# One activation table set at the head of the program instead of two in turn: a prefix log-sum-exp scan on one core

## The chip, the core and the metric

The kernel runs on one core of one Trainium2 chip. The metric is the device time of one execution in microseconds, as the median of several runs. ScalarE is called ACT here, VectorE DVE, TensorE PE (PEld for its weight loads), GpSimd POOL, SyncE SP; ACTq and SPq are the instruction queues of ACT and SP where they issue transfers.

## The reference

For each of 8 batches and 2048 columns, the output at row t is the log-sum-exp of the input rows 0 to t:

```python
B, S, D = (8, 4096, 2048)
out[:, 0, :] = x[:, 0, :]
for t in range(1, S):
    mx = np.maximum(out[:, t - 1, :], x[:, t, :])
    out[:, t, :] = mx + np.log(np.exp(out[:, t - 1, :] - mx) + np.exp(x[:, t, :] - mx))
```

Input and output are float32, 268.4 MB each.

## The kernel before, in words

The kernel takes exp of the input, makes running sums over rows with matmuls against triangular matrices of ones, and takes the logarithm of the sums. A block is 256 rows of one batch: 128 partitions with two neighbouring rows each, so a tile of 128 x 4096 numbers, 2 MB in float32. There are 16 blocks in a batch and 128 in all. The outer loop goes over pairs of batches, the middle loop over the 16 blocks, and the inner loop alternates between the two batches of the pair, each with its own running sum in PSUM (`ps`, 128 x 2048 float32).

One block goes through these steps, with the line numbers of the profile:

- L58: SP issues the load of the block into `xt` (pool of four buffers).
- L61: ACT takes Exp of all 4096 columns of `xt` into `et` (bf16, four buffers). When it is done, the `xt` buffer is free and SP can issue a load into it.
- L65 and L69: PE adds the sums up to each even row to `ps`, four pairs of matmuls of 128 x 512.
- L75: ACT takes Ln of `ps` into the first half of `ot` (float32, four buffers), the even rows.
- L76: DVE adds the odd rows' `et` to `ps` and writes the second half of `ot`.
- L77: ACT takes Ln of that half in place.
- L79: ACT issues the store of the block from `ot`. An `ot` buffer is free again when its store has landed.
- L84 and L88: PE adds the rest of the block to `ps`, so that `ps` carries the sum over the whole block. It waits for L76, which reads `ps` before.

The four triangular matrices `Li`, `Ls`, `Ui` and `Us` are made once by POOL.

ACT works in order. The order of its instructions is set by the tile scheduler when the program is built; in the middle of the program it repeats every three blocks. It ends with the last Exp, the store of the third block from the end, Ln of `ps` for the last two blocks, and then Ln in place and the store for each of the two. Exp and Ln are taken from different activation table sets in this program, so an ACT_TABLE_LOAD stands wherever ACT goes from one function to the other. These loads are not written in the source; they carry the line of the ACTIVATE behind them.

Of the kernel before, what the change touches and what calls it, by code (L numbers as in the profile page):

```python
# [1 line left out]

# [4 lines left out]


@with_exitstack
def kernel(  # L10
    ctx: ExitStack,
    tc: tile.TileContext,
    x: bass.AP,
    out: bass.AP,
):
    nc = tc.nc
    f32 = mybir.dt.float32
    bf16 = mybir.dt.bfloat16
    ACT = mybir.ActivationFunctionType

    B, S, D = x.shape
    P = 128
    SB = 256
    NBLK = S // SB
    FD = 512
    NC = D // FD
    PAIR = 2

    const = ctx.enter_context(tc.tile_pool(name="const", bufs=1))
    Li = const.tile([P, P], bf16)  # L30
    masks.make_upper_triangular(nc, Li, val=1.0, diag=True)
    Ls = const.tile([P, P], bf16)
    masks.make_upper_triangular(nc, Ls, val=1.0, diag=False)
    Ui = const.tile([P, P], bf16)
    masks.make_lower_triangular(nc, Ui, val=1.0, diag=False)
    Us = const.tile([P, P], bf16)
    masks.make_lower_triangular(nc, Us, val=1.0, diag=True)

    xpool = ctx.enter_context(tc.tile_pool(name="xpool", bufs=4))
    epool = ctx.enter_context(tc.tile_pool(name="epool", bufs=4))  # L40
    opool = ctx.enter_context(tc.tile_pool(name="opool", bufs=4))
    ppool = ctx.enter_context(tc.tile_pool(name="ppool", bufs=1, space=bass.MemoryType.PSUM))

    x_v = x.rearrange("b (k p two) d -> b k p (two d)", p=P, two=2)
    o_v = out.rearrange("b (k p two) d -> b k p (two d)", p=P, two=2)

    for bp in range(0, B, PAIR):
        psums = [
            ppool.tile([P, D], f32, name=f"ps_{bp}_{j}", tag=f"ps{j}")
            for j in range(PAIR)  # L50
        ]
        for k in range(NBLK):
            for j in range(PAIR):
                b = bp + j
                ps = psums[j]

                xt = xpool.tile([P, 2 * D], f32)
                nc.sync.dma_start(out=xt, in_=x_v[b, k])  # L58

                et = epool.tile([P, 2 * D], bf16)  # L60
                nc.scalar.activation(et, xt, ACT.Exp)  # L61

                for c in range(NC):
                    lo, hi = c * FD, (c + 1) * FD
                    nc.tensor.matmul(  # L65
                        ps[:, lo:hi], Li, et[:, lo:hi],
                        start=(k == 0), stop=False, skip_group_check=True,
                    )
                    nc.tensor.matmul(  # L69
                        ps[:, lo:hi], Ls, et[:, D + lo : D + hi],  # L70
                        start=False, stop=False, skip_group_check=True,
                    )

                ot = opool.tile([P, 2 * D], f32)
                nc.scalar.activation(ot[:, :D], ps, ACT.Ln)  # L75
                nc.vector.tensor_add(ot[:, D:], ps, et[:, D:])  # L76
                nc.scalar.activation(ot[:, D:], ot[:, D:], ACT.Ln)  # L77

                nc.scalar.dma_start(out=o_v[b, k], in_=ot)  # L79

                if k < NBLK - 1:
                    for c in range(NC):
                        lo, hi = c * FD, (c + 1) * FD
                        nc.tensor.matmul(  # L84
                            ps[:, lo:hi], Ui, et[:, lo:hi],
                            start=False, stop=False, skip_group_check=True,
                        )
                        nc.tensor.matmul(  # L88
                            ps[:, lo:hi], Us, et[:, D + lo : D + hi],
                            start=False, stop=False, skip_group_check=True,  # L90
                        )


# [1 line left out]
_INS = ['x']  # L95
_OUTS = [((8, 4096, 2048), 'float32')]


# [23 lines left out]
```

## Time and profile before

| | |
|---|---|
| time, median of 3 runs | 1329.4 us (1328.58 to 1329.96) |
| span of the profiled execution | 1326.9 us |
| ACT busy | 1268.8 us, 96% |
| PE busy | 654.6 us, 49% |
| DVE busy | 289.3 us, 22% |
| moved between HBM and SBUF | 537.22 MB, 405 GB/s over the span |
| share of the 16 DMA engines: loads, stores | 51.4%, 47.3% |

The span goes from the first to the last instruction of one profiled execution. The three timed runs lie 1.7 to 3.1 us above it. In the groups of the profile, a row gives the line, the engine, the operation, output and inputs with their shapes, the count, the busy time with the mean duration of one, and then the idle time of the engine just before them with what ended it. In the windows view, a row gives a stretch of the span, the busy time of each engine with its count of instructions in brackets, then the granted PE clock, the busy share of the DMA engines, and GB/s. A DMA engine counts as busy while a packet of its own is under way, however long that packet takes.

### The profile page before, as it was taken

The page shows a single profiled execution, that of the slowest core. Times are in us where ns is not written, and L with a number is a line of the kernel's source. Part 1 is how long each engine was busy: PE and PEld are TensorE (multiplying, and loading weights), DVE is VectorE, ACT ScalarE, POOL GpSimd, SP SyncE. Part 2 cuts the span into 40 slices and gives each one's busy share as a digit, 9 for nine tenths or more (in the row PEclk, how much of TensorE's full clock was granted, in tenths as well). Part 3 has the DMA queues.
Part 4 walks back from the last instruction along what each step waited for, and adds up shares of the span by engine and source line. Part 5 has one row for each costly group of instructions (what it writes and reads, how often), then busy time and mean ns, then how long its engine had stood idle before and what let it go on. Part 6 is the DMA issues. An engine that isn't in the chain of part 4 may idle for free.

```text
span 1326.9 us, 5421 instructions
## 1 busy us (share of the span) xinstructions
PE 654.6 (49%) x1945; PEld 244.5 (18%) x1984; DVE 289.3 (22%) x128; ACT 1268.8 (96%) x638; POOL 1.9 (0%) x12
## 2 busy tenths in 40 slices
PE   4455544544454445544454555444544455555442
PEld 1111211211121111211111221111211121122110
DVE  1222222222222222222222222222222222222222
ACT  7999999999999999999999999999999999999996
POOL 0000000000000000000000000000000000000000
PEclk9777777777777777777677777777777777777776
DMA  9999999999999999999999999999999999999976
GB/s 397 424 414 408 413 414 411 413 412 412 411 409 410 404 400 414 409 413 411 414 412 410 409 417 399 414 397 412 413 412 409 414 407 414 410 411 410 408 326 277
DMA packets 36890, 537.22 MB, mean 405 GB/s; under 512 B 4096, under 2 KB 4096, under 8 KB 4096
## 3 DMA queue, kind: packets, MB, share of 16 engines
q1 hardware_dynamic: 18432, 268.44, 51.4%
q10 hardware_dynamic: 18432, 268.44, 47.3%
q8 instruction: 15, 0.25, 0.1%
q14 instruction: 11, 0.09, 0.0%
HBM read 268.44 MB, written 268.44 MB: 405 GB/s over the span
## 4 chain that ended last, share of the span: by engine, by line
ACT 83%; PE 10%; issue 4%; ACTq 1%; DMA 1%; DVE 0%; another core or an unknown queue 0%; SPq 0%
ACT et L61 35%; ACT ot L77 18%; ACT ot L75 12%; ACT L61 9%; ACT L77 8%; PE ps L65 6%; PE ps L69 4%; ACTq L79 1%; DMA xt<-in_x_dram 1%; ACT L75 0%; DVE ot L76 0%; ACTq L75 0%; SPq L58 0%
## 5 line engine op out<-in xcount | busy, mean ns | idle before, releaser
L76 DVE TENSOR_TENSOR ot<-ps,et 128x2048 f32<-128x2048 f32 x128 | 289.3, 2288 | 1025.7 <-ACT ot L75 1025.7
L61 ACT ACTIVATE et<-xt 128x4096 bf16<-128x4096 f32 x128 | 462.9, 3617 | 9.1 <-DMA xt<-in_x_dram 7.7
L84 PE MATMUL ps<-et,Ui 128*128 128x512 bf16 x480 | 261.3, 544 | 387.7 <-DVE ot L76 385.2
L65 PE MATMUL ps<-et,Li 128*128 128x512 bf16 x512 | 245.3, 479 | 268.4 <-ACT et L61 266.3
L75 ACT ACTIVATE ot<-ps 128x2048 f32<-128x2048 f32 x128 | 240.3, 1877 | 32.4 <-ACT ot L77 19.7
L88 PE MATMUL ps<-et,Us 128*128 128x512 bf16 x463 | 254.3, 549 | 0.0
L77 ACT ACTIVATE ot<-ot 128x2048 f32<-128x2048 f32 x128 | 239.8, 1904 | 1.6 <-DVE ot L76 0.6
L69 PE MATMUL ps<-et,Ls 128*128 128x512 bf16 x490 | 224.6, 458 | 0.0
L61 ACT ACT_TABLE_LOAD x127 | 162.9, 1283 | 3.1 <-PEq L106 0.8
L88 PEld LDWEIGHTS <-Us 128*128 128x128 bf16 x480 | 61.5, 128 | 499.3 <-issue 485.2
L69 PEld LDWEIGHTS <-Ls 128*128 128x128 bf16 x512 | 59.8, 117 | 360.8 <-issue 328.1
L77 ACT ACT_TABLE_LOAD x84 | 107.8, 1283 | 1.5
L84 PEld LDWEIGHTS <-Ui 128*128 128x128 bf16 x480 | 63.4, 132 | 107.9 <-issue 93.5
L65 PEld LDWEIGHTS <-Li 128*128 128x128 bf16 x512 | 59.8, 117 | 97.6 <-issue 60.6
L75 ACT ACT_TABLE_LOAD x43 | 55.2, 1283 | 0.7
masks.py:102 POOL TENSOR_SCALAR_AFFINE_SELECT Ui<-Ui 128x128 bf16<-128x128 bf16 x1 | 0.3, 299 | 0.0
masks.py:102 POOL TENSOR_SCALAR_AFFINE_SELECT Us<-Us 128x128 bf16<-128x128 bf16 x1 | 0.3, 298 | 0.0
masks.py:66 POOL TENSOR_SCALAR_AFFINE_SELECT Ls<-Ls 128x128 bf16<-128x128 bf16 x1 | 0.3, 297 | 0.0
masks.py:66 POOL TENSOR_SCALAR_AFFINE_SELECT Li<-Li 128x128 bf16<-128x128 bf16 x1 | 0.3, 296 | 0.0
masks.py:101 POOL MEMSET Ui<- 128x128 bf16 x1 | 0.2, 208 | 0.0
masks.py:101 POOL MEMSET Us<- 128x128 bf16 x1 | 0.2, 208 | 0.0
masks.py:65 POOL MEMSET Ls<- 128x128 bf16 x1 | 0.2, 206 | 0.0
(5 smaller groups left out, 0.6 us busy)
## 6 DMA issues: line engine op xcount, KB each, us to landing
xt<-in_x_dram SPq DMA_DIRECT2D x128, 2048.0 KB, 13.6
out_dram<-ot ACTq DMA_DIRECT2D x128, 2048.0 KB, 17.3
```

The lines of the kernel that those rows point to most:

```text
L61: nc.scalar.activation(et, xt, ACT.Exp)
L65: nc.tensor.matmul(ps[:, lo:hi], Li, et[:, lo:hi], start=(k == 0), stop=False, skip_group_check=True,)
L69: nc.tensor.matmul(ps[:, lo:hi], Ls, et[:, D + lo : D + hi], start=False, stop=False, skip_group_check=True,)
L75: nc.scalar.activation(ot[:, :D], ps, ACT.Ln)
L76: nc.vector.tensor_add(ot[:, D:], ps, et[:, D:])
L77: nc.scalar.activation(ot[:, D:], ot[:, D:], ACT.Ln)
L79: nc.scalar.dma_start(out=o_v[b, k], in_=ot)
L84: nc.tensor.matmul(ps[:, lo:hi], Ui, et[:, lo:hi], start=False, stop=False, skip_group_check=True,)
L88: nc.tensor.matmul(ps[:, lo:hi], Us, et[:, D + lo : D + hi], start=False, stop=False, skip_group_check=True,)
```

## The change

One line is added at the top of the function. It loads the activation table set that holds both Exp and Ln. The builder then finds the needed function in the active set at every ACTIVATE and puts no further load into the program.

```diff
     nc = tc.nc
+    nc.scalar.preload_act_table_set("natural_log_exp_and_others")
     f32 = mybir.dt.float32
```

All lines behind it have a number one higher in the changed kernel. ACT has 254 ACT_TABLE_LOADs before and one after. On ACT, DVE and SP the remaining instructions stand in the same order in both programs, and so do PE's.

At the head of the program, ACT's rows before are these (`et` from `xt` is Exp; `ot` from `ps` and `ot` from `ot` are Ln; the two `ps` are the running sums of the two batches of a pair):

```order
L61 ACT_TABLE_LOAD
L61 ACTIVATE et<-xt 128x4096 x2
L75 ACT_TABLE_LOAD
L75 ACTIVATE ot<-ps_0_86 128x2048
L75 ACTIVATE ot<-ps_1_87 128x2048
L61 ACT_TABLE_LOAD
L61 ACTIVATE et<-xt 128x4096
```

And now:

```order
L17 ACT_TABLE_LOAD
L62 ACTIVATE et<-xt 128x4096 x2
L76 ACTIVATE ot<-ps_0_87 128x2048
L76 ACTIVATE ot<-ps_1_88 128x2048
L62 ACTIVATE et<-xt 128x4096
```

The first load stays where it was and names another set; those behind it are gone.

In the middle of the program, from one Ln of `ps` to the next Exp but one, ACT's rows before are:

```order
L75 ACT_TABLE_LOAD
L75 ACTIVATE ot<-ps_0_86 128x2048
L75 ACTIVATE ot<-ps_1_87 128x2048
L61 ACT_TABLE_LOAD
L61 ACTIVATE et<-xt 128x4096
L77 ACT_TABLE_LOAD
L77 ACTIVATE ot<-ot 128x2048 x2
L79 DMA out_dram<-ot 128x4096 x2
L75 ACTIVATE ot<-ps_0_86 128x2048
L61 ACT_TABLE_LOAD
L61 ACTIVATE et<-xt 128x4096
```

And now:

```order
L76 ACTIVATE ot<-ps_0_87 128x2048
L76 ACTIVATE ot<-ps_1_88 128x2048
L62 ACTIVATE et<-xt 128x4096
L78 ACTIVATE ot<-ot 128x2048 x2
L80 DMA out_dram<-ot 128x4096 x2
L76 ACTIVATE ot<-ps_0_87 128x2048
L62 ACTIVATE et<-xt 128x4096
```

Four loads are gone from this piece, and six from each three blocks; nothing else has moved.

## The prediction, made before the changed kernel ran

> **What bounds the kernel now.** I read the page first: the busy shares, then the DMA engines.
>
> ```profile
> span 1326.9 us, 5421 instructions
> PE 654.6 (49%) x1945; PEld 244.5 (18%) x1984; DVE 289.3 (22%) x128; ACT 1268.8 (96%) x638; POOL 1.9 (0%) x12
> DMA packets 36890, 537.22 MB, mean 405 GB/s; under 512 B 4096, under 2 KB 4096, under 8 KB 4096
> q1 hardware_dynamic: 18432, 268.44, 51.4%
> q10 hardware_dynamic: 18432, 268.44, 47.3%
> ACT 83%; PE 10%; issue 4%; ACTq 1%; DMA 1%; DVE 0%; another core or an unknown queue 0%; SPq 0%
> ```
>
> Two resources look full at once: ACT at 96%, and the DMA engines at 51.4 + 47.3 = 98.7% (q1 carries the loads, q10 the stores). Only one can set the pace. The waits of the whole span tell which:
>
> ```profile
> ACT ot L75 <- PE ps L69: 11.4, 40, 0.4
> ACT et L61 <- DMA xt<-in_x_dram: 7.7, 2, 6.4
> SPq L58 <- ACT et L61: 1207.2, 124, 11.9
> ```
>
> ACT waited for a load twice in the whole run, 7.7 us in all, at the start. SP waited 1207.2 us for Exp to free an input buffer. So the transfers wait for ACT, not ACT for them: ACT sets the pace, and the DMA engines follow. The chain that ended last agrees, with 83% on ACT.
>
> What ACT does, by groups:
>
> ```profile
> L61 ACT ACTIVATE et<-xt 128x4096 bf16<-128x4096 f32 x128 | 462.9, 3617 | 9.1 <-DMA xt<-in_x_dram 7.7
> L75 ACT ACTIVATE ot<-ps 128x2048 f32<-128x2048 f32 x128 | 240.3, 1877 | 32.4 <-ACT ot L77 19.7
> L77 ACT ACTIVATE ot<-ot 128x2048 f32<-128x2048 f32 x128 | 239.8, 1904 | 1.6 <-DVE ot L76 0.6
> L61 ACT ACT_TABLE_LOAD x127 | 162.9, 1283 | 3.1 <-PEq L106 0.8
> L77 ACT ACT_TABLE_LOAD x84 | 107.8, 1283 | 1.5
> L75 ACT ACT_TABLE_LOAD x43 | 55.2, 1283 | 0.7
> ```
>
> The work itself is 462.9 + 240.3 + 239.8 = 943.0 us; 254 table loads of 1.283 us are 325.9 us. So the question is how much of that the DMA engines let through.
>
> **The change part by part.** *The load that stays.* Its 1.28 us stand where the first load stood, ahead of the first Exp, under the 6.4 us wait for the first `xt`. It costs nothing; without that cover it would cost 1.28 us.
>
> *The loads that go.* 253 x 1.283 = 324.6 us leave ACT. What is late next is seen in one period of ACT's timeline, with PE's first and last matmul of the block that the second Ln waits for:
>
> ```profile
> 597.17 3.62 ACT L61 ACTIVATE et<-xt 128x4096 bf16<-128x4096 f32 x1
> 600.81 1.28 ACT L75 ACT_TABLE_LOAD   x1
> 602.10 1.88 ACT L75 ACTIVATE ot<-ps 128x2048 f32<-128x2048 f32 x1
> 604.26 1.88 ACT L75 ACTIVATE ot<-ps 128x2048 f32<-128x2048 f32 x1 [0.28 <-PE ps L69]
> 606.15 1.28 ACT L61 ACT_TABLE_LOAD   x1
> 607.45 3.62 ACT L61 ACTIVATE et<-xt 128x4096 bf16<-128x4096 f32 x1
> 603.78 0.44 PE L69 MATMUL ps<-et,Ls 128*128 128x512 bf16 x1
> ```
>
> The gaps around a load are 0.02 us and less, so a load is worth its 1.283 us and no more. The load at 600.81 lies beside matmuls: the second Ln starts at 604.26, when PE is done (603.78 + 0.44). Without the load, the first Ln ends 1.28 us sooner and the second still starts at 604.26. So the 43 loads of L75, 55.2 us, turn into waits for PE. The other 210 lie on ACT's own path: the second Ln of a block has its DVE sum long before, behind a whole Exp. ACT's path without transfers would be 1326.9 - 324.6 + 55.2 = 1057 us.
>
> *Exp and Ln from the other set.* The trace shows neither in that set, so their price is bounded: below, no gain, since nothing shortens the stream of elements; above, (3617 - 1877) / 2048 = 0.85 ns per element is what both functions cost per element now, and I take the same. Against the floor of the next term, 1255 us, ACT has 1255 - 1057 = 198 us to spare, so its 943 us of work could be 21% dearer before it counted.
>
> *The transfers.* 1057 us for 537.22 MB would need 508 GB/s. What the DMA engines can do is the term that decides, and the trace has it in several states:
>
> ```profile
> 0.00:10.00 10.00, 0.00 (x0) 0.10 (x1) 0.00 (x0) 2.80 (x2) 1.88 (x12) 1.00 0.83 319
> 10.00:20.00 10.00, 6.56 (x16) 2.19 (x16) 0.00 (x0) 8.72 (x4) 0.00 (x0) 1.00 1.01 431
> 20.00:30.00 10.00, 7.50 (x26) 2.88 (x25) 4.52 (x2) 9.59 (x6) 0.00 (x0) 0.83 1.00 429
> 100.00:1260.00 1160.00, 583.04 (x1737) 218.09 (x1772) 255.37 (x113) 1125.39 (x568) 0.00 (x0) 0.77 1.00 410
> ```
>
> From 10 to 30 us, with loads alone and several queued, a share of 1.00 moves 427 to 429 GB/s (431 / 1.01). Over the middle of the program the share is 1.00 too, but it moves 410. Two stretches of one period, each with the queues' own shares, show where the difference lies. From 604 to 609 us loads and stores run side by side:
>
> ```profile
> DMA packets 149, 2.16 MB, mean 433 GB/s; under 512 B 17, under 2 KB 17, under 8 KB 17
> q10 hardware_dynamic: 72, 1.16, 54.3%
> q1 hardware_dynamic: 77, 1.00, 46.8%
> ```
>
> From 612 to 617 us the stores have run out, and ACT issues the next ones only from 614.32:
>
> ```profile
> 614.32 2.14 ACTq L79 DMA_DIRECT2D out_dram<-ot  x2
> DMA packets 137, 1.90 MB, mean 380 GB/s; under 512 B 21, under 2 KB 21, under 8 KB 21
> q1 hardware_dynamic: 131, 1.88, 100.4%
> ```
>
> Side by side: 433 / 1.011 = 428 GB/s per full share, the same as loads alone with a deep queue. With one load draining and nothing behind it: 380, at a share of 100%. So the share of 1.00 hides slow packets, and these stand where ACT has not yet released the next transfer. I take 428 GB/s as the cap, since it is what both directions together reach (nearest to what comes), and 380 as the lower end of what could persist.
>
> With ACT needing 1057 us and the transfers more, ACT will wait: for a load in front of Exp, or for a landed store where Ln needs an `ot` buffer. In either case it waits for a transfer under way, and up to four loads and up to four stores can be queued (four buffers each), so a lone draining load should become rare. Behind a waiting Ln on ACT stand the next Exp, so the next `xt` is freed later, and the next store's issue; loads then drain while stores have the engines, and the wait ends sooner. The floor is 537.22 MB / 428 GB/s = 1255.2 us.
>
> [...]
>
> *The edges.* The first 10 us moved 319 GB/s where 428 were possible: 10 x (1 - 319 / 428) = 2.5 us lost, unchanged. At the end, the last blocks go through ACT with nothing to load; here are the last Exp, the issue of the last store, and the times that stores took from issue to landing:
>
> ```profile
> 1303.73 3.62 ACT L61 ACTIVATE et<-xt 128x4096 bf16<-128x4096 f32 x1
> 1317.16 0.34 ACTq L79 DMA_DIRECT2D out_dram<-ot  x1
> DMA to landing us min/median/max: 6.3/17.3/19.8
> ```
>
> From the last Exp to the last store's issue it is 13.4 us now, with one table load in it whose place PE's matmuls for that block take, so about 13, and the last store lands 6.3 us later at the least: 20 us at the earliest, and up to 23 us if it queues behind another, after the last load has landed. In these 20 to 23 us the engines have three stores to do that cannot have been issued before (the last three blocks are stored behind the last Exp), 3 x 2.097 MB / 428 = 14.7 us, and what was queued before, none to two of 4.9 us each. So 0 to 8 us are lost there; I take 5.
>
> *What may stay of slow packets.* The middle's 410 instead of 428 is worth 537.22 x (1/410 - 1/428) = 55 us over the run. Between none and half of it (27 us) may stay; I take 5, since a queue that holds work on both sides showed none.
>
> *Sum.* 1255.2 + 2.5 + 5 + 5 = 1268 us of span. The median of the three runs, 1329.4, lies 2.5 us above the profiled span of 1326.9; with as much on top, the time is 1270 us.
>
> **The rivals.** (1) *The DMA engines are full already.* The share of 1.00 in the middle means what it says, and slow reads belong to this traffic, not to a queue that runs dry. Then all of 537.22 MB go at 410: 1310 + 2.5 + 5 + 2.5 = 1320 us, and 1292 us if half of the slow packets go. For it: share 1.00 over 1160 us. Against it: SP's 1207 us of waiting for ACT, and 428 side by side.
>
> (2) *Slower: loads and stores in each other's way.* With ACT no longer pacing them, both queues are full all the time, and HBM serves the two directions together below 407 GB/s: 537.22 / 407 + 7.5 = 1327 us is the point from which it decides. At 380, the lowest sustained rate at full share, it would be 1414 + 7.5 + 2.5 = 1424 us. Against it: 433 GB/s from 604 to 609 us with both queues busy. [...]
>
> (3) *No cap at 428.* ACT and PE set the time: 1057 + 2.5 = 1060 us. For it: over the middle ACT asked for no more than 410. Against it: loads alone and both directions together stop at the same 428.
>
> (4) *The loads come back*, if the set lacked a function: 1329 us. The built program has one load.
>
> **How the numbers follow.** Forecast 0.79, rival (1) 0.13, (2) 0.04, (3) 0.02, (4) 0.02. No change can be told from the runs' own spread below about 0.2%, 2.7 us. Faster by more: 0.79 + 0.13 + 0.02 = 0.94. Within: 0.02. Slower: 0.04. The range takes the forecast's own bounds: at the low end 1249 (at 430 GB/s, since shares and rates are rounded) + 2.5 + 0 + 0 + 2.5 = 1254 us; at the high end 1255 + 2.5 + 5 + 27 + 2.5 = 1292 us, which meets the better half of rival (1). What is left out holds 2 in 10 at most.
>
> **What would show it.** In the profile of the changed kernel: one ACT_TABLE_LOAD; ACT's busy time near 944 us, with Exp at 3617 ns and the two Ln at 1877 and 1904; ACT's waits led by loads or by landed stores, some 250 us and more in all; waits for PE at the first Ln near 50 us or hidden under those for transfers; the middle at 424 to 428 GB/s with a share of 1.00; loads and stores side by side in nearly every stretch; 20 to 23 us from the last Exp's start to the end. The forecast is wrong if the middle stays near 410 GB/s (rival 1), falls below it (2), or exceeds 435 (3).

## The result and the profile after

The changed kernel takes 1259.32 us (1259.15 to 1259.64) against 1329.68 us (1328.58 to 1330.13) before: a ratio of 0.9473 (95% interval 0.946 to 0.9486), 70 us less. The forecast was 1270 us in a range of 1254 to 1292. The profiled execution has a span of 1257.6 us; its time was 1259.34.

The page after, in the rows that answer to those of before:

```profile
span 1257.6 us, 5168 instructions
PE 645.3 (51%) x1945; PEld 239.4 (19%) x1984; DVE 293.0 (23%) x128; ACT 915.9 (73%) x385; POOL 1.9 (0%) x12
DMA packets 36888, 537.21 MB, mean 427 GB/s; under 512 B 4096, under 2 KB 4096, under 8 KB 4096
q1 hardware_dynamic: 18432, 268.44, 50.0%
q10 hardware_dynamic: 18432, 268.44, 49.9%
q8 instruction: 15, 0.25, 0.1%
DMA 71%; ACT 26%; PE 1%; issue 1%; DVE 0%; ACTq 0%; SPq 0%
```

ACT fell from 96% busy to 73%, and the chain that ended last went from 83% ACT to 71% DMA. Loads and stores now take the same engine time for the same bytes: the loads took 51.4% of 1326.9 = 682 us before and take 50.0% of 1257.6 = 629 us now. What went are the slow packets.

The groups of ACT, then its waits over the whole span:

```profile
L76 ACT ACTIVATE ot<-ps 128x2048 f32<-128x2048 f32 x128 | 239.8, 1873 | 319.2 <-DMA out_dram<-ot 284.9
L62 ACT ACTIVATE et<-xt 128x4096 bf16<-128x4096 f32 x128 | 461.7, 3607 | 7.9 <-DMA xt<-in_x_dram 7.9
L78 ACT ACTIVATE ot<-ot 128x2048 f32<-128x2048 f32 x128 | 238.9, 1899 | 0.7 <-DVE ot L77 0.7
L17 ACT ACT_TABLE_LOAD x1 | 1.3, 1283 | 0.8 <-PEq L107 0.8
```

```profile
ACT ot L76 <- DMA out_dram<-ot: 284.9, 56, 7.8
ACT ot L76 <- PE ps L70: 32.6, 28, 1.8
ACT et L62 <- DMA xt<-in_x_dram: 7.9, 2, 6.6
```

One table load is left. Exp and Ln cost in the common set what they cost before (3607 and 3617 ns, 1873 and 1877, 1899 and 1904). ACT's new wait is for landed stores: 56 times in front of a Ln that needs an `ot` buffer, 285 us. It never waits for a load after the first two.

The windows of the head and of the middle, and the queues' shares from 612 to 617 us, where before only loads ran at 380 GB/s:

```profile
0.00:10.00 10.00, 0.00 (x0) 0.10 (x1) 0.00 (x0) 2.57 (x2) 1.86 (x12) 1.00 0.83 315
100.00:1200.00 1100.00, 572.41 (x1709) 211.77 (x1744) 258.92 (x113) 805.98 (x339) 0.00 (x0) 0.74 1.01 431
DMA packets 150, 2.20 MB, mean 439 GB/s; under 512 B 16, under 2 KB 16, under 8 KB 16
q1 hardware_dynamic: 71, 1.15, 53.5%
q10 hardware_dynamic: 79, 1.05, 49.1%
```

Both directions run side by side, and the middle moves 431 GB/s where it moved 410. One period of ACT shows where the freed time went:

```profile
598.36 1.88 ACT L76 ACTIVATE ot<-ps 128x2048 f32<-128x2048 f32 x1 [6.19 <-DMA out_dram<-ot]
600.13 3.61 ACT L62 ACTIVATE et<-xt 128x4096 bf16<-128x4096 f32 x1
...
627.70 1.88 ACT L76 ACTIVATE ot<-ps 128x2048 f32<-128x2048 f32 x1 [7.11 <-DMA out_dram<-ot]
```

From one long wait to the next it is 29.3 us for three blocks, 9.8 us each, which is two transfers of 2.097 MB at 430 GB/s. Mind also the starts: the Exp at 600.13 begins before the Ln of 598.36 has ended (600.24). Neighbouring ACTIVATEs overlap by 0.1 us here; in the rows of before, with a load between them, they did not: 0.01 to 0.02 us lie on either side of each load.

### The profile page after: what moved, and what is told of

Same layout as the page of the kernel before. It is cut to its first block, busy times and chain, and to the rows that moved or that the text cites. A ratio compares the mean times of both kernels' runs of the same rounds, so it can differ in the third digit from the quotient of the medians.

```text
span 1257.6 us, 5168 instructions
## 1 busy us (share of the span) xinstructions
PE 645.3 (51%) x1945; PEld 239.4 (19%) x1984; DVE 293.0 (23%) x128; ACT 915.9 (73%) x385; POOL 1.9 (0%) x12
## 2 busy tenths in 40 slices
DMA packets 36888, 537.21 MB, mean 427 GB/s; under 512 B 4096, under 2 KB 4096, under 8 KB 4096
## 3 DMA queue, kind: packets, MB, share of 16 engines
q1 hardware_dynamic: 18432, 268.44, 50.0%
q10 hardware_dynamic: 18432, 268.44, 49.9%
HBM read 268.44 MB, written 268.44 MB: 427 GB/s over the span
## 4 chain that ended last, share of the span: by engine, by line
DMA 71%; ACT 26%; PE 1%; issue 1%; DVE 0%; ACTq 0%; SPq 0%
DMA out_dram<-ot 70%; ACT et L62 13%; ACT ot L76 7%; ACT ot L78 7%; DMA xt<-in_x_dram 1%; DVE ot L77 0%; PE ps L66 0%; PE ps L70 0%; PE ps L85 0%; PE ps L89 0%; ACTq L76 0%; ACTq L80 0%; SPq L59 0%
## 5 line engine op out<-in xcount | busy, mean ns | idle before, releaser
L85 PE MATMUL ps<-et,Ui 128*128 128x512 bf16 x480 | 265.4, 553 | 511.6 <-DVE ot L77 509.2
L77 DVE TENSOR_TENSOR ot<-ps,et 128x2048 f32<-128x2048 f32 x128 | 293.0, 2291 | 949.4 <-ACT ot L76 949.4
L76 ACT ACTIVATE ot<-ps 128x2048 f32<-128x2048 f32 x128 | 239.8, 1873 | 319.2 <-DMA out_dram<-ot 284.9
L62 ACT ACTIVATE et<-xt 128x4096 bf16<-128x4096 f32 x128 | 461.7, 3607 | 7.9 <-DMA xt<-in_x_dram 7.9
L66 PE MATMUL ps<-et,Li 128*128 128x512 bf16 x512 | 228.0, 445 | 81.2 <-ACT et L62 79.6
L89 PE MATMUL ps<-et,Us 128*128 128x512 bf16 x463 | 261.9, 566 | 0.0
L78 ACT ACTIVATE ot<-ot 128x2048 f32<-128x2048 f32 x128 | 238.9, 1899 | 0.7 <-DVE ot L77 0.7
L70 PE MATMUL ps<-et,Ls 128*128 128x512 bf16 x490 | 211.0, 431 | 0.0
L66 PEld LDWEIGHTS <-Li 128*128 128x128 bf16 x512 | 59.7, 117 | 98.1 <-issue 59.6
```

The lines of the kernel that those rows point to most:

```text
L66: nc.tensor.matmul(ps[:, lo:hi], Li, et[:, lo:hi], start=(k == 0), stop=False, skip_group_check=True,)
L70: nc.tensor.matmul(ps[:, lo:hi], Ls, et[:, D + lo : D + hi], start=False, stop=False, skip_group_check=True,)
L85: nc.tensor.matmul(ps[:, lo:hi], Ui, et[:, lo:hi], start=False, stop=False, skip_group_check=True,)
L89: nc.tensor.matmul(ps[:, lo:hi], Us, et[:, D + lo : D + hi], start=False, stop=False, skip_group_check=True,)
```

## The experiments

My theory: the table loads were on ACT's path and ACT alone set the pace; without them, the transfers bind at 430 GB/s and hide most of what ACT gained. The rival: the DMA engines, with their share of 1.00, were part of the pace already, or ACT's work still adds to the time.

**Transfers alone.** Against the changed kernel, all that computes is taken out of the loop, and the input pool has eight buffers in place of four:

```diff
-                et = epool.tile([P, 2 * D], bf16)
-                nc.scalar.activation(et, xt, ACT.Exp)
...
-                nc.scalar.dma_start(out=o_v[b, k], in_=ot)
+                nc.scalar.dma_start(out=o_v[b, k], in_=xt)
```

> Leaves out all computation: each block goes from HBM into one of eight SBUF buffers and from there back to HBM, the same 537 MB in the same 2 MB transfers on the same two queues; the output is the input. Theory (the changed kernel stands at the transfers' rate of 430 GB/s with every engine): 537.2 / 430 = 1249 us plus 2.7 us at the head and some 5 to 8 us at the end, 1255 to 1262 us, within 5 us of the changed kernel. Rival (computing takes rate from the transfers): under 1245 us, with more than 433 GB/s in the middle.

Measured: 1253.7 us (1253.49 to 1254.05), a hair under the range. Its page and its middle:

```profile
span 1252.1 us, 558 instructions
100.00:1200.00 1100.00, 0.00 (x0) 0.00 (x0) 1.00 1.01 431
```

The rate is the same 431 GB/s to the last digit, with no engine computing. So the changed kernel stands 5.6 us above the transfers' own time, and computing takes no rate from them that this row would show.

**Half of the stores left out, before and after the change.** The same line in both kernels:

```diff
-                nc.scalar.dma_start(out=o_v[b, k], in_=ot)
+                nc.scalar.dma_start(out=o_v[b, k][:, D:], in_=ot[:, D:])
```

> The kernel before, storing only the odd rows (half of each output tile), so 403 MB in place of 537 MB; all computation stays. Theory (ACT alone paced the kernel before, the DMA share of 1.00 was slow packets): 1325 to 1332 us, as before. Rival (transfers shared in the pace of the kernel before): at least 15 us faster than before.

> The changed kernel, storing only the odd rows, 403 MB in place of 537 MB; all computation stays. Theory: transfers need 403 / 430 = 936 us and no longer bind, so ACT with its waits for PE sets the time: 1057 us by the prediction's sum, 25 us less for the overlap of neighbouring ACTIVATEs that the profile after shows, so 1030 to 1065 us. Then some 270 to 300 us less than the same edit of the kernel before. Rival (the removed loads were worth only what the full kernel gained, 70 us): about 1255 us.

Measured: 1324.69 us (1323.85 to 1325.27) with the table loads and 964.86 us (963.29 to 966.08) without. The kernel before, with a quarter of its bytes gone, loses 5 us of 1330. That is 0.3 us below the 1325 to 1332 that I expected, and far from the rival's 15:

```profile
q1 hardware_dynamic: 18432, 268.44, 58.3%
100.00:1260.00 1160.00, 588.99 (x1774) 218.64 (x1773) 255.38 (x113) 1125.39 (x568) 0.00 (x0) 0.77 0.84 307
1317.28 0.34 ACTq L79 DMA_DIRECT2D out_dram<-ot  x1
```

Its middle moves 307 GB/s at a share of 0.84, and the loads alone take 58.3% of 1322.1 = 771 us of engine time, 89 us more than in the full kernel. So here the busy share says little of how full the engines are: for the same loads it grew, from 682 to 771 us, when there was less to do beside them. The last row is the issue of the last store: it comes at 1317.28 us here and at 1317.16 in the full kernel. ACT got through its work in the same time, and the 5 us lie behind it, where a store of half the size lands sooner: from that issue to the end of the span it is 4.8 us here and 9.7 us in the full kernel. That ACT alone paced the kernel before is settled.

The changed kernel with half of the stores:

```profile
PE 581.0 (60%) x1984; PEld 224.1 (23%) x1984; DVE 289.5 (30%) x128; ACT 916.7 (95%) x385; POOL 1.9 (0%) x12
ACT 83%; PE 11%; issue 2%; ACTq 2%; DMA 1%; DVE 1%; SPq 0%
L76 ACT ACTIVATE ot<-ps 128x2048 f32<-128x2048 f32 x128 | 239.8, 1874 | 32.5 <-PE ps L70 21.2
L66 PE MATMUL ps<-et,Li 128*128 128x512 bf16 x512 | 215.2, 420 | 65.4 <-ACT et L62 65.0
```

ACT sets the pace here, at 963 us of span instead of the 1057 that I had worked out, and under the 1030 to 1065 that I expected of this run. The difference to the same edit before, 359.8 us, is 1.42 us for each of the 253 loads, more than the 1.283 us of a row. Two steps of my sum were off. The groups of ACT (461.7 + 239.8 + 238.9) come to 24 us more than its busy 916.7, which is the overlap. And the waits for PE are 21 us, where I had put 55 on top of the 11 of before; in all, ACT is idle for 47 us here where it was idle for 58 before. The two are nearly all of the 94 us between 1057 and 963. The matmuls of L66 took 420 ns where those of L65 took 479 in the same edit of the kernel before, at a granted clock of 0.82 in place of 0.77. One period of each shows what that does. These are the windows of the eight matmuls between an Exp and the second Ln behind it, first with the table loads, then without:

```profile
600.90:604.40 3.50, 3.38 (x8) 1.13 (x8) 0.27 (x1) 3.19 (x4) 0.00 (x0) 0.55 1.00 351
616.90:618.90 2.00, 1.89 (x8) 0.77 (x8) 0.16 (x1) 1.81 (x2) 0.00 (x0) 1.00 1.02 434
```

With the table loads PE was busy with the eight for 3.4 us, at a granted clock of 0.55; without them for 1.9 us, at 1.00. The second Ln waits 0.28 us for PE in the first case and 0.20 in the second, although the table load in front of the first Ln is gone. Why the clock was higher was not tried.

**ACT time put back, first try.** One more Exp per block:

```diff
                 nc.scalar.activation(et, xt, ACT.Exp)
+                nc.scalar.activation(et[:, 0:1344], xt[:, :1344], ACT.Exp)
```

> The changed kernel with one more Exp on each block, over 1344 columns again into the same et columns: some 1.2 to 1.3 us more ACT work per block, 128 times, about 160 us, half of what the loads took. Theory (ACT has about 200 us to spare under the transfers): 1257 to 1264 us, no more than 5 us over the changed kernel, and ACT's waits for stores shrink by about 150 us. Rival (ACT and transfers add, since ACT works in order and issues the stores): 1300 us and more.

Measured: 1436.74 us, slower than before the change. This looks like the rival, but the profile shows another cause. The wait that leads on ACT, and two rows of ACT's timeline of one block:

```profile
ACT ot L77 <- PE ps L71: 337.8, 123, 3.7
604.80 1.31 ACT L63 ACTIVATE et<-xt 128x1344 bf16<-128x1344 f32 x1
608.08 1.88 ACT L77 ACTIVATE ot<-ps 128x2048 f32<-128x2048 f32 x1 [1.98 <-PE ps L71]
```

The scheduler had put ACT's instructions in another order: the extra Exp, which PE must wait for, stands right ahead of the Ln that needs PE's result, in nearly every block. PE's time, hidden behind other ACT work in the changed kernel, lies on the path. The run alone can't tell the order from the 168 us of added work (128 times 1.31). With the next run, in which 218 us of added work cost 5, it says that the order of ACT's instructions is worth some 170 us here.

**ACT time put back, second try.** The order must stay. The first ACTIVATE only copies, and the last takes Ln of the whole tile:

```diff
-                nc.scalar.activation(ot[:, :D], ps, ACT.Ln)
+                nc.scalar.activation(ot[:, :D], ps, ACT.Copy)
...
-                nc.scalar.activation(ot[:, D:], ot[:, D:], ACT.Ln)
+                nc.scalar.activation(ot, ot, ACT.Ln)
```

> The changed kernel with two thirds of the removed ACT time put back in another form: the first ACTIVATE of each block only copies the sums into the output tile, and the last takes Ln of all 4096 columns in place of 2048, so 2048 x 0.84 = 1.7 us more per block, 219 us in all; ACT's order in the loop stays the changed kernel's, and PE gets its data no later. Theory (transfers bind; ACT's path, 963 us where half the stores were left out, has room): 963 + 219 = 1182 us is still under the transfers' 1250, so 1256 to 1266 us, with ACT's waits for stores shrunk from 285 to under 120 us. Rival (ACT's work adds to the time, as the 1437 us of the run with one more Exp could mean): over 1300 us.

Measured: 1263.96 us (1262.81 to 1265.7). ACT's busy time and its wait for stores:

```profile
PE 610.5 (48%) x1945; PEld 231.3 (18%) x1984; DVE 293.0 (23%) x128; ACT 1134.3 (90%) x385; POOL 1.9 (0%) x12
ACT ot L76 <- DMA out_dram<-ot: 89.3, 39, 3.0
```

218 us more work on ACT (1134.3 - 915.9) cost 4.6 us; the wait for stores gave 196 us of it back. So ACT had nearly all of that to spare, and the transfers hid it. The middle, from 100 to 1200 us, moves 431 GB/s in this run too; the 4.6 us stand at the end, while ACT is busy with the last blocks: the last two of the page's 40 slices move 401 and 285 GB/s here and 430 and 326 in the changed kernel.

**One load at a time.** Are slow packets a matter of a queue that runs dry, or of stores just before? One input buffer, only Exp behind it, and 8 of the 128 stores left:

```diff
-    xpool = ctx.enter_context(tc.tile_pool(name="xpool", bufs=4))
+    xpool = ctx.enter_context(tc.tile_pool(name="xpool", bufs=1))
```

> Leaves out the running sums, Ln and nearly all stores: each block is loaded and its Exp taken, with one input buffer, so the next load is issued only when Exp is done; eight blocks of exponentials are stored. Theory (a load that drains with nothing queued behind it has slow packets, whatever stores do): the 268 MB of loads take visibly more than 624 us x 428 / 430 of engine time at a share of 1.00, the share of the loads' queue comes out some 5 to 20% above bytes / 430 GB/s; about 11 us per block and 1400 to 1500 us in all. Rival (the slow packets of the kernel before came from stores just before them): the share of the loads' queue is within 2% of bytes / 430 GB/s.

Measured in a single run: 1482 us, with this load queue, and three windows of one load, which SP issues at 608.86 us:

```profile
span 1480.5 us, 587 instructions
q1 hardware_dynamic: 18432, 268.44, 50.1%
608.00:610.00 2.00, 0.00 (x0) 0.84 (x1) 0.00 (x0) 1.00 0.37 74
610.00:612.00 2.00, 0.00 (x0) 0.00 (x0) 0.00 (x0) 1.00 0.74 205
612.00:614.00 2.00, 0.00 (x0) 0.00 (x0) 0.00 (x0) 1.00 1.03 442
```

50.1% of 1480.5 is 742 us of engine time for 268.44 MB, 19% over the 624 us at 430 GB/s, with hardly a store in the program. So in this run loads by themselves have slow packets, and the stores are not needed for them. But the windows show them at another place than my theory: the first 3 us behind the issue move 200 and 277 GB/s for a full share (74 / 0.37 and 205 / 0.74), and from 612 us on, with nothing queued behind the load, it is 429 (442 / 1.03). The slow packets here are the first of this load, which starts alone, not those of its drain. The stretch of the kernel before from which I took the drain says the same, in smaller windows:

```profile
614.00:616.00 2.00, 0.00 (x0) 0.00 (x0) 0.00 (x0) 2.00 (x2) 0.00 (x0) 1.00 1.01 418
616.00:618.00 2.00, 0.00 (x0) 0.00 (x0) 0.00 (x0) 1.53 (x2) 0.00 (x0) 0.89 1.07 287
```

One load is under way here with nothing behind it. At first it moves 418 GB/s at a share of 1.01; it is slow, 287 at 1.07, from about 2 us after ACT has issued the first of two stores, at 614.32 us. In both stretches the slow packets follow the issue of a transfer while only loads move. The next two loads of the run with one load at a time begin alike: in steps of 1 us, with the busy share in tenths, the engines move 229 and 246 GB/s at 0.9 and 0.7, and 229 and 147 at 0.9 and 0.5, and in the three steps behind them 377 to 492 at 0.8 and 0.9. Whether the issue itself slows the packets was not tried.

**The end.** In the changed kernel the engines run half empty from 1240 to 1245 us, while ACT works on the last two blocks, and again at the very end:

```profile
1240.00:1245.00 5.00, 0.00 (x0) 0.00 (x0) 2.44 (x2) 3.82 (x2) 0.00 (x0) 0.62 0.57 242
1250.00:1252.00 2.00, 0.00 (x0) 0.00 (x0) 0.00 (x0) 0.00 (x0) 0.00 (x0) 0.50 0.92 393
1252.00:1254.00 2.00, 0.00 (x0) 0.00 (x0) 0.00 (x0) 0.00 (x0) 0.00 (x0) 0.50 0.37 156
1254.00:1256.00 2.00, 0.00 (x0) 0.00 (x0) 0.00 (x0) 0.00 (x0) 0.00 (x0) 0.50 0.06 25
```

I took the first gap for the cause of most of the 5.6 us over the transfers alone, and tried to fill it in two ways and in both together:

```diff
-    opool = ctx.enter_context(tc.tile_pool(name="opool", bufs=4))
+    opool = ctx.enter_context(tc.tile_pool(name="opool", bufs=6))
```

```diff
                 nc.scalar.activation(ot[:, :D], ps, ACT.Ln)
+                if k == NBLK - 1 and bp == B - PAIR:
+                    nc.sync.dma_start(out=o_v[b, k][:, :D], in_=ot[:, :D])
...
+                if k == NBLK - 1 and bp == B - PAIR:
+                    nc.sync.dma_start(out=o_v[b, k][:, D:], in_=ot[:, D:])
+                else:
+                    nc.scalar.dma_start(out=o_v[b, k], in_=ot)
```

> The changed kernel with six output buffers in place of four. Theory of the end: ACT is held back by landed stores, so when the last load has landed it still has blocks to do, and the engines ran dry for 7 us; with two more buffers ACT runs two blocks further ahead and more stores are queued at the end: 1253 to 1257 us. Rival (the end is set by the chain from the last Exp alone): 1258 to 1260 us, as the changed kernel. The middle stays at 430 GB/s in both.

> The changed kernel with the last block of each of the last two batches stored in two halves, each from SP as soon as it is computed. Theory of the end: about 5 us of the 7 us in which the engines were dry are filled by the two early halves, 1254 to 1256 us. Rival (the last stores are limited by something else, as the latency of landing): 1258 to 1260 us.

> Six output buffers and the early halves together. Theory: both fill the same dry stretch at the end, so no more than the better of the two by 2 us: 1252 to 1256 us, close to the 1253.7 us of transfers alone. Rival (they add): under 1252 us, which transfers alone did not reach.

Measured: 1259.3, 1259.64 and 1259.45 us, each within 0.4 us of the changed kernel. The theory of the end fell, three times. The gap was filled, and nothing came of it; the same stretches with both edits:

```profile
1240.00:1245.00 5.00, 0.00 (x0) 0.00 (x0) 0.73 (x1) 2.12 (x2) 0.00 (x0) 0.50 1.00 423
1250.00:1252.00 2.00, 0.00 (x0) 0.00 (x0) 0.00 (x0) 0.00 (x0) 0.00 (x0) 0.50 0.29 123
1252.00:1254.00 2.00, 0.00 (x0) 0.00 (x0) 0.00 (x0) 0.00 (x0) 0.00 (x0) 0.50 0.06 25
1254.00:1256.00 2.00, 0.00 (x0) 0.00 (x0) 0.00 (x0) 0.00 (x0) 0.00 (x0) 0.50 0.07 29
```

The bulk is done about 2 us sooner, and then 25 to 29 GB/s go on to the same end: a sixteenth of 430 is 27, so it looks as if one DMA engine of the 16 were still at work at its full rate. What does it have more of than the others? The page lists 15 packets of 16 KB of instructions (q8), which the copy, with 558 instructions, does not have. So the number of instructions was changed, in both directions:

```diff
-    FD = 512
+    FD = 256
```

```diff
-                if k < NBLK - 1:
-                    for c in range(NC):
-                        lo, hi = c * FD, (c + 1) * FD
-                        nc.tensor.matmul(
-                            ps[:, lo:hi], Ui, et[:, lo:hi],
...
-                            ps[:, lo:hi], Us, et[:, D + lo : D + hi],
```

> The changed kernel with matmuls of 256 columns in place of 512, so twice as many matmuls and weight loads, some 9140 instructions in place of 5168; ACT's order and all transfers of data stay. Theory (the end is set by one DMA engine that also fetches the instructions: in the last 4 to 5 us of the changed kernel the 16 engines together move 16 to 33 GB/s, a sixteenth of 430): about 12 more fetches of 16 KB at 0.6 to 0.9 us each, so 7 to 11 us more, 1266 to 1270 us, with the lone engine running 12 us and more after the others. Rival (the end is set by something common to every run, as landing and closing): 1258 to 1261 us.

> The changed kernel without the 960 matmuls of the upper triangles and their weight loads, so that no sum is carried on to the next block; 3248 instructions in place of 5168, ACT's order and all transfers of data stay. Theory (one engine also fetches the instructions): about 6 fetches of 16 KB fewer, 4 to 5 us, and no lower than transfers alone at 1253.7 us: 1253 to 1256 us. Rival (the end is common to every run): 1258 to 1261 us.

Measured: 1263.54 us (1263.01 to 1264.19) with twice the matmuls, 1256.91 us (1256.63 to 1257.16) without the upper ones. Both directions are as the theory has them, and both sizes are short of it. The instruction rows of the two, and the lone engine in the first:

```profile
span 1262.1 us, 9175 instructions
q8 instruction: 31, 0.51, 0.1%
1256.00:1258.00 2.00, 0.00 (x0) 0.00 (x0) 0.00 (x0) 0.00 (x0) 0.00 (x0) 0.50 0.92 393
1258.00:1260.00 2.00, 0.00 (x0) 0.00 (x0) 0.00 (x0) 0.00 (x0) 0.00 (x0) 0.50 0.06 25
```

```profile
span 1255.1 us, 3287 instructions
q8 instruction: 8, 0.13, 0.0%
```

With 0, 8, 15 and 31 such packets the spans are 1252.1, 1255.1, 1257.6 and 1262.1 us: 0.38, 0.36 and 0.28 us for each more, about half of what I had put on one engine. That the span grows with the number of packets is shown, in these four kernels. That the packets cause it is not: the copy has no ACT work behind its last load, and the other two have half or twice the matmuls too. With twice the matmuls the lone engine works for some 3 us after the others, as in the changed kernel, and not for the 12 us and more that I expected. ACT's last Exp starts at 1237.82 us there and at 1232.54 in the changed kernel, so the delay has come up before the end. Without the upper matmuls the lone engine is gone (213 GB/s from 1252 to 1254 us, then nothing). Whether the packets all lie on the engine that ends last, no run shows.

**A version with fewer matmuls.** DVE adds the two rows of a partition once, and PE sums that:

```diff
+                st = spool.tile([P, D], bf16)
+                nc.vector.tensor_add(st, et[:, :D], et[:, D:])
...
+                        ps[:, lo:hi], Ls, st[:, lo:hi],
...
+                nc.vector.tensor_add(ot[:, :D], ps, et[:, :D])
+                nc.vector.tensor_add(ot[:, D:], ps, st)
+                nc.scalar.activation(ot, ot, ACT.Ln)
...
+                            ps[:, lo:hi], Us, st[:, lo:hi],
```

> A whole kernel with half the matmuls: DVE adds the two rows of a partition once, PE takes the strictly lower and the upper triangle of that sum (8 matmuls per block in place of 16), DVE adds the block's own rows to the sums, and ACT takes one Ln of 4096 columns per block. Theory of the fetching engine: some 6 to 7 fetches fewer, 1253 to 1257 us, if its bursts (five Exp and then five Ln in turn) leave both queues fed. Rival: the bursts let one queue run dry, slow packets come back and the middle falls under 425 GB/s, 1262 us and more.

Measured: 1257.8 us (1256.9 to 1258.71), a ratio of 0.9462 (0.9449 to 0.9474) to the kernel before. All its runs lie under all runs of the changed kernel, by 1.5 us at the medians, but the intervals of the two ratios overlap. It is at best 0.1% better than the changed kernel. Its middle moves 431 GB/s, so the rival's slow packets stayed away, but it ends a hair above the 1253 to 1257 us of the theory: it has 7 packets of instructions, one fewer than the kernel without the upper matmuls, and takes 0.9 us longer. Transfers alone are 4 us below it, and no version beat that.

## Why the prediction was right

- *ACT alone sets the pace before, the share of 1.00 notwithstanding.* Right, and shown by the run with half of the stores.
- *The transfers hide most of ACT's gain.* Right: without the table loads ACT could do with 360 us less, and the full kernel gained 70.
- *The cap, 428 GB/s.* Right in kind, 3 GB/s low: the middle moves 431, which makes the floor 537.21 / 431 = 1246 us and not 1255. This is the largest error of the sum, 9 us. I divided the 431 and 433 GB/s of short stretches by their shares of 1.01, as if a share ended at 1.00. The middle of the changed kernel has 1.01 too, so the rate as it stood was the cap: 431 stands over 1100 us, in a run that loads and stores 268.44 MB each.
- *Slow packets, 5 us of up to 27.* None to speak of stayed (629 us of engine time for the loads, as for the stores). But the place that I gave them was wrong: I put them where one load drains with nothing behind it, and the run with one load at a time shows them behind the issue of a transfer, where only loads move (200 and 277 GB/s for a full share), and the drain at full rate (429). That they go when both queues hold work is true by either account, so the small term came out right with half of its reason wrong.
- *ACT's path without transfers, 1057 us.* Wrong by some 94 us, without effect on the time. The step that failed is "the 43 loads of L75, 55.2 us, turn into waits for PE": they did not (11 us of waiting for PE became 21), as PE's matmuls did not keep the pace that I had left them at, and the overlap of ACTIVATEs was missing from the sum.
- *What ACT waits for.* I left open whether loads or stores; it is stores alone with four output buffers. With six it waits for loads, above all (151.0 us in 82 waits in front of Exp), and the time is the same.
- *The edges.* The head was right (315 GB/s in the first 10 us). For the end I took 5 us out of 0 to 8, and the rates give 7: 5 x (1 - 242 / 431) = 2.2 us from 1240 to 1245, then 0.2, 1.3 and 1.9 in the three stretches from 1250 on, and 1.6 behind them; but the step behind it, that the chain from the last Exp on sets the end in 20 to 23 us, failed: it took 25.1 us (1232.54 to 1257.6), two ways of feeding the engines sooner changed nothing, the time went with the number of instructions, and what sets the end stays open.
- *The time over the span*, 2.5 us, was 1.7. I had taken the median of three executions over the span of another; most executions lie 1.7 to 1.8 us above their own span.

Put together, the measured terms would lower the sum by 9 + 5 + 0.8 - 2 = 13 us; the time came out 10.7 us lower. The 2 us between stay unassigned.

## What to carry to other kernels

When two resources look full, ask who waits for whom: here the waits said ACT, and a part of the DMA share of 1.00 was slow packets. Before removing work from the engine that paces, work out the next cap from the best stretch of the trace, since here that, and not the 360 us that ACT could do without, gave the gain of 70. And an experiment that adds work must leave the order as it is, or it measures the order: 1437 us with 168 us of work added and another order, 1264 with 218 us added and the same order.

## What was not expected of the hardware

A table load cost 1.42 us on ACT's path rather than the 1.283 us of its row, as the two kernels with half of the stores show: of the 35 us between 253 x 1.283 and 359.8, 24 are the overlap of neighbouring ACTIVATEs, which with a load between them was not there. In the run with one load at a time, the loads of 2 MB took 19% more engine time than their bytes at 430 GB/s (742 us in place of 624), and in the load followed there the first packets were the slow ones (200 and 277 GB/s for a full share, then 429). And the span of four kernels that are bound by their transfers grew with the instructions that were fetched: 1252.1 us without packets of 16 KB, 1262.1 with 31; that the fetches are the cause is not shown.
